# Hybrid decoder block: four rows a visit in the dense stage, a shorter lag, and five edits ahead of it

## The chip, the cores and the metric

The kernel runs on one core of one Trainium2 chip. The metric is device microseconds of one execution, the median of the runs. An execution that the hardware profiler recorded gives the trace; its own time and span stand in the table below. Times in the trace are microseconds from the start of the span.

The engines are called TensorE (PE, and PEld for its weight loads), VectorE (DVE), ScalarE (ACT), GpSimd (POOL) and SyncE (SP); the last three also issue transfers.

## The reference

The layer has 1024 tokens of width 1024, in two sub-layers. Everything is float32.

```python
h = modulate(rms_norm(x, n1_pre), shift1, scale1)
proj = h @ w_in                       # conv gates, q, k, v, o, i, f, g_A, g_B
ya = (b_gate * causal_conv(c_gate * x_in)) @ w_branch_a
ym = (sigmoid(o) * head_norm(mlstm(q, k, v, i, f)) * w) @ w_branch_m
y = (sigmoid(g_A) * ya + sigmoid(g_B) * ym) @ w_out
x = x + gate1 * rms_norm(y, n1_post)

h = modulate(rms_norm(x, n2_pre), shift2, scale2)
q = h @ wq                            # 8 heads, two halves of 128 each
s1, i1 = top_k(q[..., 0] @ subkeys0, 16)      # of 128 keys
s2, i2 = top_k(q[..., 1] @ subkeys1, 16)
sc, e = top_k(all sums s1 + s2, 16)           # 16 of 128 x 128 experts, per head
a = gelu(u[e] . h) * softmax(sc)              # 8 x 16 experts per token
x = x + gate2 * rms_norm(sum_e a_e * v[e], n2_post)
```

u and v are tables of 16384 rows of 1024 values. Each token needs 128 rows of each.

## The kernel before

The tokens stand in two halves of 512. Each goes through the mixer (sub-layer 1) and the scores (query projections and the choice of keys); then the two halves take different roads through the experts. For the first half, rows of u and v are gathered from the tables by indirect transfers. For the second half the experts are computed densely: all 16384 rows of u are projected, the activations are multiplied by a gate matrix G that is zero where a token hasn't chosen an expert, and all rows of v are multiplied with the result.

In time: set-up, the first half's mixer, from 583 us its eight output projections "O", the norm, the first half's scores; from 845 us the second half's mixer with the gathers of the first half underneath; the output projections of the second half end near 1488; a tail with the norm until 1545; the second half's scores until 1752, which also compute 10 of the 40 dense u projections that are done ahead ("az", stored to `A_d`); the selection for the first dense block and the building of the gates (`gates_block`, stored to `G_d`) until 2093; then the dense stage to the end.

**A projection** (`proj_w`, L263) is a group of 24 wide matmuls. A float32 product is split in three passes: high by high, high by low, low by high (L268, L269, L273). `halves` (L246) loads 512 KB of weights into `wr`, ScalarE makes the high part `wh` (L257) and VectorE the low part `wl` (L259). After each matmul `pump` advances the background generator of gathers by `rate[0]` units per projection: RATE1 2.6 at first, RATEM 2 in the middle, RATE1B 4.5 from the M projections of the second half on, RATE2 2.8 and RATE3 3.2 in dense.

**The gathers** (`gather_stream`, L908) alternate u units and v units. A unit issues one indirect transfer of 128 table rows, 512 KB, on POOL's queue (L900 for u, L872 for v) into a buffer that `row_tile` gives: a ring of seven, in the dense stage with three more. `step` keeps the uses in a list and lets the oldest go when what is behind is more than `lag[0]` (LAG 5, in dense LAGD 8). A u use is one VectorE instruction (L905) that multiplies the rows with `h2n` and sums them into a column of `z`. A v use is a visit of TensorE: eight matmul records a row (L891), in four column groups of the array, added into `acc`. v rows are held until `nvs[0]` of them have been issued and then used in one visit: one row per unit would be 1, NVA 2 applies before dense and NV 2 in dense.

```python
            held.append((s, blocks[b].issue_v(s)))
            if len(held) >= nvs[0] or s % 32 == 31:
                step(len(held), lambda z=tuple(held): [blocks[b].use_v(*y) for y in z][-1])
                held.clear()
```

**The order of the work.** Outside dense a list scheduler orders each engine's instructions by their dependences. In dense the order on TensorE, VectorE and ScalarE is written out by hand. There 64 groups of two expert rows each take the rest of the u projections (88), the gelu, the gate from `G_d`, and three passes of v (L1258 to L1260), eight tiles per group; the gather units are pumped in between.

**The mixer's end.** After the last A projection `during(8)` computes the second half's first norm (`norm_mod`: per channel group one scaling, L364, a ScalarE copy, and one subtraction, L368), then VectorE makes `mxh`/`mxl` (L669), the input of the eight O projections. For each O the result is squared (`squares`) and multiplied with the residual input `x2` (`cross`, two projections behind); both are summed by small matmuls into one tile. `turned_sums` (L321) turns the sums, L705 copies them to `m` behind the last issued u use (`last_u`), and the norm goes on.

**The spilled gates.** Eight "gm" projections of the second half are made early, in the first half's tail, where `filler` needs TensorE work, and stored to `spill`. In the second half `gate` loads one into a `t512` buffer (a ring of four of 2 KB) for each of the eight M projections.

**The selection** (`select`, L757) takes for the eight heads the 16 best sums of 50 candidates: adds into `cd`, then per head two rounds of maximum and index (L770 to L776), then turns positions into expert numbers (L803 to L821). `gates_prep` and `gates_block` make one-hots (L1059, L1062), multiply them on TensorE (L1068) and store G. `z_ahead` (L1020) makes the early dense u projections into a buffer "az" that shares tag `W`, of two buffers, with others.

## Time and profile before

| what | value |
|---|---|
| time, median of 3 runs | 3551.16 us (3549.02 to 3554.36) |
| the profiled execution's own time | 3540.15 us |
| its span in the trace | 3538.0 us |
| mean granted clock of TensorE | 0.963 |
| TensorE busy | 3287.7 us, 93% |
| VectorE busy | 2569.6 us, 73% |
| ScalarE busy | 1113.7 us, 31% |
| GpSimd busy | 1182.9 us, 33% |
| moved by transfers | 928.99 MB, mean 263 GB/s |

Busy time is the time in which an engine executes something. Matmuls overlap, so the length printed for one is longer than the distance to the next; the starts are what counts. [...] A page's share is a mean over stages, and what a change is worth is read from the stage in which it is made.

### The profile page before, as it was taken

Reading aid. Unit: us, or ns where it says so; the run is one execution under the profiler, and the core shown is the slowest. Engines: PE = TensorE matmul, PEld = TensorE weight load, DVE = VectorE, ACT = ScalarE, POOL = GpSimd, SP = SyncE. Lnnn points to the kernel's source line nnn. Section 1 sums busy time; section 2 is a strip of 40 time slices with the busy share of each in tenths; the row PEclk is TensorE's granted clock in tenths of the full one; section 3 lists DMA queues with packets and bytes.
Section 4 is the critical chain, followed back from the end, with each engine's and each line's share of the span. In section 5 each row is a group of like instructions: output and inputs, shape, how many; then the busy total and the mean of one; then the engine's idle time right before and its main releaser. Section 6 shows DMA issues by size and latency. Waiting matters only on the chain.

```text
span 3538.0 us, 49527 instructions
## 1 busy us (share of the span) xinstructions
PE 3287.7 (93%) x18208; PEld 2438.1 (69%) x18208; DVE 2569.6 (73%) x6003; ACT 1113.7 (31%) x1831; POOL 1182.9 (33%) x1040
## 2 busy tenths in 40 slices
PE   8999999999988899879968789999999999999997
PEld 5777877686766666446656667777777777776665
DVE  5362444489899886688899848888887888775546
ACT  4442333334332222222256542222222222222221
POOL 0000000001416666546411114544535544444441
PEclk9999999999989899989989899999999999999999
DMA  4226323243739999979957798999989999999994
GB/s 169 84 96 220 121 83 102 83 147 99 276 102 358 333 374 380 355 269 364 345 181 217 217 299 327 352 347 350 344 291 351 349 354 349 352 336 329 320 332 148
DMA packets 326307, 928.99 MB, mean 263 GB/s; under 512 B 35248, under 2 KB 109232, under 8 KB 323888
## 3 DMA queue, kind: packets, MB, share of 16 engines
q0 software_dynamic: 147456, 536.94, 41.5%
q1 hardware_dynamic: 103984, 336.38, 27.1%
q10 hardware_dynamic: 74624, 52.51, 4.8%
q8 instruction: 142, 2.33, 0.3%
q14 instruction: 101, 0.83, 0.1%
HBM read 869.09 MB, written 56.63 MB: 262 GB/s over the span
## 4 chain that ended last, share of the span: by engine, by line
PE 75%; DVE 13%; DMA 5%; issue 3%; ACT 2%; POOL 1%; ACTq 0%; SPq 0%; DVEq 0%; POOLq 0%
PE pj L268 15%; PE pj L269 14%; PE pj L273 14%; PE pa L891 7%; PE pj L1258 5%; PE pj L1259 5%; PE pj L1260 5%; DVE ug L905 2%; PE pm L1258 2%; DMA vg<-in_v_tab_dram,eT 2%; PE pm L1259 2%; PE pm L1260 2%; DVE wl L259 1%; ACT gst L1070 1%; DMA wr<-in_w_in_dram 1%
## 5 line engine op out<-in xcount | busy, mean ns | idle before, releaser
L900 POOL DMA_INDIRECT ug<-in_u_tab_dram,ei x512 | 612.6, 1196 | 1480.6 <-DVE eT L850 869.1
L268 PE MATMUL pj<-hhi,wh 128*128 128x512 f32 x2320 | 950.8, 411 | 39.2 <-ACT wh L257 24.0
L269 PE MATMUL pj<-hlo,wh 128*128 128x512 f32 x2320 | 924.0, 399 | 2.5 <-DVE hlo L368 2.1
L872 POOL DMA_INDIRECT vg<-in_v_tab_dram,eT x512 | 560.8, 1095 | 812.6 <-PE pa L891 513.7
L259 DVE TENSOR_TENSOR wl<-wr,wh 128x512 fp32r<-128x512 f32 x502 | 342.8, 688 | 419.6 <-PE pj L273 352.8
L905 DVE CUSTOM_DVE_ANT_0 ug<-ug,h2n 128x1024 f32<-128x1024 f32 x512 | 615.3, 1222 | 11.5 <-DMA ug<-in_u_tab_dram,ei 9.4
L273 PE MATMUL pj<-hhi,wl 128*128 128x512 f32 x2320 | 600.8, 398 | 6.7 <-DVE wl L259 6.7
L268 PEld LDWEIGHTS pj<-hhi,wh 128*128 128x128 f32 x2320 | 444.6, 192 | 201.7 <-issue 52.8
L257 ACT CAST wh<-wr 128x512 fp32r<-128x512 f32 x502 | 308.7, 621 | 795.5 <-PE pj L269 431.9
L273 PEld LDWEIGHTS pj<-hhi,wl 128*128 128x128 f32 x2320 | 439.6, 191 | 121.2 <-issue 16.4
L269 PEld LDWEIGHTS pj<-hlo,wh 128*128 128x128 f32 x2320 | 445.3, 192 | 101.2 <-DVE hlo L368 8.8
L1242 DVE TENSOR_TENSOR dacc<-dacc,pj 128x512 f32<-128x512 f32 x378 | 256.2, 685 | 297.9 <-PE pj L1260 297.1
L1258 PE MATMUL pj<-Vk,Ak 128*128 128x512 f32 x768 | 308.3, 401 | 11.2 <-ACT Ak L1156 11.1
L891 PE MATMUL pa<-vg,dgm 128*32 128x256 f32 x4096 | 291.5, 390 | 25.7 <-DMA vg<-in_v_tab_dram,eT 23.2
L1260 PE MATMUL pj<-Vk,Ak 128*128 128x512 f32 x768 | 300.1, 391 | 4.1 <-DVE Ak L1159 4.1
L1259 PE MATMUL pj<-Vk,Ak 128*128 128x512 f32 x768 | 301.3, 392 | 0.0
L891 PEld LDWEIGHTS pa<-vg,dgm 128*32 128x32 f32 x4096 | 103.8, 109 | 170.7 <-issue 81.1
L1146 ACT ACTIVATE a<-pj 128x512 f32<-128x512 f32 x88 | 52.6, 598 | 498.1 <-PE pj L273 498.0
L1258 PEld LDWEIGHTS pj<-Vk,Ak 128*128 128x128 f32 x768 | 144.2, 188 | 68.3 <-issue 21.0
L1156 ACT CAST Ak<-a 128x512 fp32r<-128x512 f32 x128 | 79.5, 621 | 353.2 <-DVE a L1154 337.7
L1126 ACT CAST Vk<-vr 128x1024 fp32r<-128x1024 f32 x128 | 134.3, 1049 | 139.6 <-PE pj L1260 128.6
L1260 PEld LDWEIGHTS pj<-Vk,Ak 128*128 128x128 f32 x768 | 144.5, 188 | 37.4 <-DVE Ak L1159 6.1
(324 smaller groups left out, 4145.2 us busy)
## 6 DMA issues: line engine op xcount, KB each, us to landing
wr<-in_w_in_dram SPq DMA_DIRECT2D x128, 512.0 KB, 4.1
wr<-in_uT_dram SPq DMA_DIRECT2D x128, 512.0 KB, 6.2
vr<-in_v_tab_dram SPq DMA_DIRECT2D x128, 512.0 KB, 6.8
gt<-G_d SPq DMA_DIRECT2D x64, 512.0 KB, 8.3
G_d<-gst ACTq DMA_DIRECT2D x15, 2048.0 KB, 11.1
wada<-in_w_ada_dram SPq DMA_DIRECT2D x12, 2048.0 KB, 8.3
wr<-in_wq_dram SPq DMA_DIRECT2D x32, 512.0 KB, 4.1
A_d<-az ACTq DMA_DIRECT2D x40, 256.0 KB, 4.9
```

The costliest lines, as they stand in the source:

```text
L257: S.copy(hi, part)
L259: V.tensor_sub(lo, part, hi.bitcast(F32))
L268: PE.matmul(p, wh, xh[:, dc, :], start=(dc == 0), stop=False)
L269: last_pe[0] = PE.matmul(p, wh, xl[:, dc, :], start=False, stop=False)
L273: last_pe[0] = PE.matmul(p, wl, xh[:, dc, :], start=False, stop=(dc == ND - 1))
L872: G.indirect_dma_start(out=vg, out_offset=None, in_=v_tab, in_offset=bass.IndirectOffsetOnAxis(ap=self.eT[:, t:t + 1], axis=0))
L891: i = PE.matmul(self.acc[32 * q:32 * q + 32, 0:256], self.dgm[t // 8][:, t % 8, :], vg[:, 256 * q:256 * q + 256], start=(tau == 0), stop=( ...
L900: G.indirect_dma_start(out=ug, out_offset=None, in_=u_tab, in_offset=bass.IndirectOffsetOnAxis(ap=self.ei[:, s:s + 1], axis=0))
L905: last_u[0] = order(V.tensor_tensor_reduce(out=ug, in0=ug, in1=self.h2n, scale=1.0, scalar=0.0, op0=OP.mult, op1=OP.add, accum_out=self.z[ ...
L1258: PE.matmul(p, A[:, 0, bs], Vk[:, 0, ds_], start=(i1 == 2 * g), stop=False)
L1259: PE.matmul(p, A[:, 0, bs], Vk[:, 1, ds_], start=False, stop=False)
L1260: PE.matmul(p, A[:, 1, bs], Vk[:, 0, ds_], start=False, stop=(i1 == 2 * g + 1))
```

## The change

Seven edits, of which the first concerns the dense stage and the others the way to it.

1. NV goes from 2 to 4 and LAGD from 8 to 6: in dense four v rows are held and used in one visit, and uses follow six units behind.
2. The two small set-up tiles `diff` and `qd` take buffers of tag `W` in place of `t512`.
3. `norm_mod` gets its loop body as `piece`. The second half's norm no longer stands whole ahead of `mxh`/`mxl`: the O projections 0 to 3 of the first half each take two pieces behind them. In the first half `x2` is loaded after O projection 3 and all eight `cross` come after the last one.
4. The spilled gates are loaded two at a time straight into `u`, ahead of the M projections, in place of one each into `t512`.
5. The rate of the gathers is zero in the last O projection of the second half, and RATE1B again behind it.
6. The selection for the first dense block is made in two halves of four heads (`parts=2`). It is begun in the second half's scores at step 8 and advanced through step 12; the rest follows the scores as before.
7. The "az" buffers are three of their own, in the room of `Cst` (two) and `rstd` (one), in place of two of `W`.

```diff
-NV = 2
+NV = 4
-LAGD = 8
+LAGD = 6
...
+    diff = sp.tile([128, 128], I32, name="diff", tag="W", bufs=2)
-    diff = sp.tile([128, 128], I32, name="diff", tag="t512", bufs=4)
...
-    qd = sp.tile([128, 4, 32], I32, name="qd", tag="t512", bufs=4)
+    qd = sp.tile([128, 4, 32], I32, name="qd", tag="W", bufs=2)
...
-    def norm_mod(x, r, A, sh, keep, in_big=False, first=None):
+    def norm_pieces(x, r, A, sh, keep, in_big=False):
...
-        for dc in range(ND):
-            if first:
-                first(dc)
+
+        def piece(dc):
             s_ = sh[:, dc:dc + 1]
             t = sp.tile([128, TH], F32, name="nm", tag="t512", bufs=4)
             V.scalar_tensor_tensor(t, x[:, dc, :], A[:, dc:dc + 1], r, op0=OP.mult, op1=OP.mult)
...
+        return (hi, lo), hf, piece
...
-        if hf == 1 and (kind, j) in FILL0:
-            nc.sync.dma_start(t, spill[FILL0.index((kind, j))])
-            return t
...
         u = big([128, ND, TH], F32, "u")
+        if hf == 1:
+            for j in range(0, ND, 2):
+                nc.sync.dma_start(u[:, j:j + 2], spill[j:j + 2].rearrange("j p t -> p j t"))
         for j in range(ND):
             wa = ada_load(4 + j) if hf == 0 else None
-            t = gate("gm", j, h, hf)
+            t = gate("gm", j, h, hf) if hf == 0 else u[:, j, :]
...
-        during(8)
         mxh = big([128, ND, TH], F32R, "mxh")
...
-        x2 = big([128, ND, TH], F32, "x2")
-        nc.sync.dma_start(x2, xT[hf])
+        x2s = []
+
+        def x2_load():
+            x2s.append(big([128, ND, TH], F32, "x2"))
+            nc.sync.dma_start(x2s[0], xT[hf])
+
+        if hf == 1:
+            x2_load()
...
         for j in range(ND):
+            if hf == 1 and j == ND - 1:
+                rate[0] = 0.0
             S.copy(y[:, j, :], proj("O", j, (mxh, mxl)))
             squares(j)
-            if j > 1:
+            during(ND + j)
+            if hf == 0 and j == 3:
+                x2_load()
+            if hf == 1 and j > 1:
                 cross(j - 2)
-        cross(ND - 2)
-        cross(ND - 1)
+        if hf == 1:
+            rate[0] = RATE1B
+        for j in range(0 if hf == 0 else ND - 2, ND):
+            cross(j)
...
-    def select(tv, ti, c, res, kind=""):
+    def select(tv, ti, c, res, kind="", parts=1):
...
+        n = H // parts
+        for h0 in range(0, H, n):
+            hs, js = slice(h0, h0 + n), slice(2 * h0, 2 * h0 + 2 * n)
+            V.tensor_copy(i_bf[:, js], ti[:, c, js])
...
+            for hd in range(h0, h0 + n):
+                V.max(sv[:, hd, 0:8], cd[:, hd, :])
+                V.max_index(po[:, hd, 0:8], sv[:, hd, 0:8], cd[:, hd, :])
+                yield 1
...
+            if h0 + n < H:
+                yield 1
...
-            a = sp.tile([128, TD], F32, name="az", tag="W", bufs=2)
+            if not zz:
+                zz.append(sp.tile([128, 2, TD], F32, name="zz", tag="Cst", bufs=1))
+                zz.append(sp.tile([128, 1, TD], F32, name="zy", tag="rstd", bufs=RSB))
+            a = (zz[0][:, 0], zz[0][:, 1], zz[1][:, 0])[n % 3]
...
     def during(j):
...
-        if j == 8:
-            nxt.append(norm_mod(*nxt[0], A1, sh1, False)[0])
+        if j == ND:
+            nxt.extend(norm_pieces(*nxt[0], A1, sh1, False))
+        if ND <= j < ND + 4:
+            nxt[3](2 * (j - ND))
+            nxt[3](2 * (j - ND) + 1)
...
+        if not NX and j == H:
+            chosen.append(select(tv, ti, 0, res0, "d", 2))
+        if not NX and H <= j < H + H // 2 + 1:
+            next(chosen[0])
...
-        for n, _ in enumerate(select(tv, ti, 0, res, "d")):
-            z_ahead(h2, ZT[0] + (ZT[1] - ZT[0]) * (n + 1) / (H + 3))
-        building.append(gates_block(0, *gates_prep(*res)))
+        for n, _ in enumerate(chosen[0]):
+            z_ahead(h2, ZT[0] + (ZT[1] - ZT[0]) * (n + 1) / (H // 2 + 3))
+        building.append(gates_block(0, *gates_prep(*res0)))
```

## Rows read from the trace of the kernel before

**Rows 1.** Busy time on the page: engine, us, share of span, instructions.

```profile
PE 3287.7 (93%) x18208; PEld 2438.1 (69%) x18208; DVE 2569.6 (73%) x6003; ACT 1113.7 (31%) x1831; POOL 1182.9 (33%) x1040
```

**Rows 2.** Windows by stage: busy us of each engine, clock, DMA share, GB/s.

```profile
2150.00:3450.00 1300.00, 1290.58 (x7370) 953.84 (x7369) 982.95 (x1775) 328.69 (x502) 614.20 (x559) 1.00 0.93 340
2660.00:3140.00 480.00, 480.00 (x2676) 359.85 (x2672) 389.43 (x697) 126.61 (x192) 236.10 (x212) 1.00 0.95 350
...
1350.00:1450.00 100.00, 97.41 (x553) 61.68 (x552) 63.78 (x122) 24.95 (x42) 58.66 (x56) 1.00 1.01 388
582.00:600.00 18.00, 10.68 (x35) 7.91 (x34) 14.73 (x24) 8.63 (x15) 0.00 (x0) 0.72 0.39 146
1490.00:1546.00 56.00, 32.65 (x144) 14.34 (x141) 41.22 (x92) 8.57 (x14) 21.88 (x19) 0.70 0.54 183
1545.00:1752.00 207.00, 191.94 (x1179) 136.43 (x1179) 179.63 (x725) 51.01 (x88) 127.32 (x109) 0.99 0.98 366
...
2093.00:2123.00 30.00, 18.91 (x90) 13.04 (x89) 11.42 (x19) 7.93 (x12) 4.95 (x6) 0.77 0.89 334
```

**Rows 3.** Timeline of TensorE around a two-row visit in dense: start, length.

```profile
2281.31 0.39 PE L1259 MATMUL pj<-Vk,Ak 128*128 128x512 f32 x1
...
2282.22 0.39 PE L1260 MATMUL pj<-Vk,Ak 128*128 128x512 f32 x1
2282.54 1.07 PE L891 MATMUL pa<-vg,dgm 128*32 128x256 f32 x16
...
2284.82 0.39 PE L1260 MATMUL pj<-Vk,Ak 128*128 128x512 f32 x1
```

**Rows 4.** Timeline of TensorE around a one-row visit.

```profile
1481.46 0.39 PE L268 MATMUL pj<-mxh,wh 128*128 128x512 f32 x1
1481.78 0.64 PE L891 MATMUL pa<-vg,dgm 128*32 128x256 f32 x8
...
1483.85 0.40 PE L269 MATMUL pj<-mxl,wh 128*128 128x512 f32 x1
```

**Rows 5.** Windows of line L891 alone: the use of v rows in dense.

```profile
2150.00:3450.00 1300.00, 172.38 (x2576) 67.28 (x2576) 1.00 0.93 340
2105.00:3500.00 1395.00, 187.16 (x2784) 72.87 (x2784) 0.99 0.92 333
```

**Rows 6.** DMA issues, 2660 to 3140: count, median us from issue to landing.

```profile
ug<-in_u_tab_dram,ei POOLq DMA_INDIRECT x106, 7.0
vg<-in_v_tab_dram,eT POOLq DMA_INDIRECT x106, 7.3
```

**Rows 7.** Timeline of VectorE at the first half's output projections.

```profile
586.64 2.08 DVE L364 SCALAR_TENSOR_TENSOR nm<-xt,A,rstd 128x512 f32<-128x512 f32 x3
...
590.62 4.91 DVE L669 SCALAR_TENSOR_TENSOR mxl<-u,mxh 128x512 fp32r<-128x512 f32 x8
```

**Rows 8.** Timeline of TensorE there; in brackets idle before, and its releaser.

```profile
587.39 0.80 PE L268 MATMUL pj<-mxh,wh 128*128 128x512 f32 x1 [4.14 <-ACT wh L257]
591.36 0.79 PE L269 MATMUL pj<-mxl,wh 128*128 128x512 f32 x1 [3.17 <-DVE mxl L669]
```

**Rows 9.** Chain of waits through the second mixer's end: start, length, what.

```profile
1490.85 3.12 PE pm L690 x6
...
1494.68 1.05 PE pm L321 x8
```

**Rows 10.** Timeline of VectorE at the same place.

```profile
1506.50 1.23 DVE L905 CUSTOM_DVE_ANT_0 ug<-ug,h2n 128x1024 f32<-128x1024 f32 x1 [3.42 <-DMA ug<-in_u_tab_dram,ei]
...
1507.65 0.17 DVE L705 COPY m<-pm 128x12 f32<-128x12 f32 x1
```

**Rows 11.** Timeline of TensorE at the first dense block's selection.

```profile
1789.24 0.69 PE L1039 MATMUL pm<-ident,e 128*128 128x128 f32 x2 [11.68 <-DVE e L821]
...
1795.50 0.58 PE L1068 MATMUL pj<-oh 128*128 128x128 f16 x4 [4.96 <-DVE oh L1062]
```

**Rows 12.** Waits from 1800 to 2110: total us, times, longest.

```profile
DVE ge L803 <- DMA A_d<-az: 9.7, 3, 5.9
```

More of the change, by code (lines that the diff above doesn't have):

```diff
@@ L355, in norm_mod @@
         else:
[L356 to L357 removed]
+            hi, lo = (hp_.tile([128, ND, TD], F32R, name=n, tag="h") for n in ("hhi", "hlo"))
         hf = big([128, ND, TH], F32, "hf") if keep else None
[L359 to L361 removed]
+        def piece(dc):
             s_ = sh[:, dc:dc + 1]
@@ L368, in norm_mod @@
             V.scalar_tensor_tensor(lo[:, dc, :], t, s_, hi[:, dc, :].bitcast(F32), op0=OP.add, op1=OP.subtract)
-        return (hi, lo) if in_big else whole, hf
+        return (hi, lo), hf, piece
+    def norm_mod(x, r, A, sh, keep, in_big=False, first=None):
+        whole, hf, piece = norm_pieces(x, r, A, sh, keep, in_big)
+        for dc in range(ND):
+            if first:
+                first(dc)
+            piece(dc)
+        return whole, hf
     def x_rms(hf):
@@ L755, in scores @@
                 V.max_index(ti[:, c, j, 8:16], tv[:, c, j, 8:16], r)
-    def select(tv, ti, c, res, kind=""):
+    def select(tv, ti, c, res, kind="", parts=1):
         i_bf = sp.tile([128, 2 * H, TOPK], BF, name="i_bf", tag="i_bf")
-        V.tensor_copy(i_bf, ti[:, c])
-        s1, s2 = tv[:, c, 0::2, :], tv[:, c, 1::2, :]
         cd = sp.tile([128, H, NCAND], F32, name="cd", tag="cd")
-        for a in range(8):
-            V.tensor_add(cd[:, :, OFF[a]:OFF[a + 1]], s2[:, :, 0:CNT[a]],
-                         s1[:, :, a:a + 1].to_broadcast([128, H, CNT[a]]))
-        V.tensor_add(cd[:, :, OFF[8]:NCAND], s1[:, :, 8:16], s2[:, :, 0:1].to_broadcast([128, H, 8]))
@@ L767, in select @@
         sv = sp.tile([128, H, TOPK], F32, name="sv", tag="sv")
         po = sp.tile([128, H, TOPK], U32, name="po", tag="po")
-        for hd in range(H):
-            V.max(sv[:, hd, 0:8], cd[:, hd, :])
-            V.max_index(po[:, hd, 0:8], sv[:, hd, 0:8], cd[:, hd, :])
-            yield 1
-            r = sp.tile([128, NCAND], F32, name="mr2", tag="mr2")
-            V.match_replace(r, sv[:, hd, 0:8], cd[:, hd, :], NEG)
-            V.max(sv[:, hd, 8:16], r)
-            V.max_index(po[:, hd, 8:16], sv[:, hd, 8:16], r)
+        n = H // parts
@@ new lines, in select @@
+        for h0 in range(0, H, n):
+            hs, js = slice(h0, h0 + n), slice(2 * h0, 2 * h0 + 2 * n)
+            V.tensor_copy(i_bf[:, js], ti[:, c, js])
+            s1, s2 = tv[:, c, 2 * h0:2 * h0 + 2 * n:2, :], tv[:, c, 2 * h0 + 1:2 * h0 + 2 * n:2, :]
+            for a in range(8):
+                V.tensor_add(cd[:, hs, OFF[a]:OFF[a + 1]], s2[:, :, 0:CNT[a]],
+                             s1[:, :, a:a + 1].to_broadcast([128, n, CNT[a]]))
+            V.tensor_add(cd[:, hs, OFF[8]:NCAND], s1[:, :, 8:16], s2[:, :, 0:1].to_broadcast([128, n, 8]))
+            for hd in range(h0, h0 + n):
+                V.max(sv[:, hd, 0:8], cd[:, hd, :])
+                V.max_index(po[:, hd, 0:8], sv[:, hd, 0:8], cd[:, hd, :])
+                yield 1
+                r = sp.tile([128, NCAND], F32, name="mr2", tag="mr2")
+                V.match_replace(r, sv[:, hd, 0:8], cd[:, hd, :], NEG)
+                V.max(sv[:, hd, 8:16], r)
+                V.max_index(po[:, hd, 8:16], sv[:, hd, 8:16], r)
+            if h0 + n < H:
+                yield 1
@@ L1009, in block_kernel @@
     A_d = dr.tile([max(ZA, 1), 128, TD], F32, name="A_d")
-    ahead = [0]
+    ahead, zz = [0], []
     NC = -(-TD // TH)
@@ L1324, in filler @@
             gate(*z, h, keep=True)
-    h2, tv, ti = stage1(0, h, lambda h2, j: None, during, filler)
+    h2, tv, ti = stage1(0, h, lambda *z: None, during, filler)
     blocks = []
@@ L1343, in block_kernel, with second @@
     rate[0], mix[0] = RATE1, MIX1
-    building = []
-    def second(h2, j):
+    building, chosen, res0 = [], [], []
+    def second(h2, j, tv, ti):
         z_ahead(h2, ZT[0] * j / 16.0)
+        if not NX and j == H:
+            chosen.append(select(tv, ti, 0, res0, "d", 2))
+        if not NX and H <= j < H + H // 2 + 1:
+            next(chosen[0])
         if NX and j == 4:
```

10 lines of the change are left out of this document (4 added, 6 removed).

## The prediction

> **What bounds the kernel now.** I read the page's busy times first: TensorE is busy in 93% of the span [rows 1]. That is a mean over stages, so the table of windows by stage comes next [rows 2]. In the dense stretch from 2150 to 3450 us TensorE is busy for 1290.58 of 1300 us at a granted clock of 1.00, while the DMA engines stand at a share of 0.93 and 340 GB/s. Between 2660 and 3140 it has no gap at all, and VectorE works 389.43 of 480 us. So in 37% of the span only less TensorE time makes the kernel shorter; nothing that another engine saves there counts. The other windows are the places where TensorE waits and where the clock is granted at half: 582 to 600 (first half's output projections begin), 1490 to 1546 (end of the second mixer) and 2093 to 2123 (dense begins). There it is waits that count, and the timeline around each says which one ends last.
>
> **Four v rows a visit.** In dense every visit to the `acc` accumulation breaks the sequence of wide matmuls. The timeline of a two-row visit shows the price [rows 3]: wide matmuls start every 0.227 us ((2282.22 - 2281.31)/4), and the six steps from 2282.22 to 2284.82 take 2.60 us, where six regular ones take 1.36. The visit costs 1.24 us. A one-row visit [rows 4]: seven steps from 1481.46 to 1483.85 take 2.39 us, regular 1.59, so 0.80. The difference, 0.44, is a row; what is left, 0.36, is paid per visit however many rows it has. Dense has 2784 such matmuls [rows 5], 8 records to a row: 348 rows, 174 visits now, 87 after. 87 x 0.36 = 31.3 us, of which 2576/2784 lie where TensorE is full: 29.0. Reading the row's price as 0.41 or 0.48 moves the fixed part between 0.28 and 0.42, hence 22 to 34 us. I take -29.
>
> [...]
>
> The price of it is in the queue. A visit now waits for the last of four transfers, and the lag falls from eight to six. Tiles in flight are at most ten (six behind plus four held), the ten `row_tile` buffers. Behind a visit of four, u units are used as few as four units after their issue, against eight before. A unit passes every 480/212 = 2.26 us (106 u and 106 v, [rows 6]), so four are 9.1 us. From issue to landing a u row takes 7.0 us and a v row 7.3 (the same rows). The margin is about 2 us, and a late u stalls VectorE, not TensorE. VectorE has 480 - 389.43 = 90.6 us free for 106 u rows, 0.85 us each, before it becomes the bound. I take nothing for it; rival C has the other end.
>
> **First half's output projections.** Now `during(8)` puts sixteen norm instructions of VectorE (three take 2.08 us, [rows 7]) ahead of `mxh`/`mxl`. TensorE stands 4.14 and then 3.17 us, the second wait ending with `mxl` [rows 8]. In the window of 18 us 35 matmuls start, at a mean clock of 0.72 [rows 2]; at 0.227 us apart they need 7.9, so 10 us are lost. With the norm in pieces behind the O steps, 2 x 2 x 0.69 = 2.8 us of VectorE a step hide under a projection of 24 x 0.227 = 5.4 us. `mxl` stays ahead of the second matmul (8 x 0.61 us, [rows 7]), so some 3 us remain lost: -7. If the scheduler orders the wait elsewhere, 0.
>
> The other end of that stage gets longer. `x2` is loaded at j == 3, so all eight `cross` come after the last projection: a pass cost 3.12/6 = 0.52 us at half clock [rows 9], two of the eight stood there already, and six less 1 us that leaves the loop is +2. Net -5, from -9 to 0.
>
> **Spilled gates in place.** Eight loads of 256 KB become four of 512 KB into `u`, issued before the M projections. The u buffer is free only when what had its slot is read; the loads replace a `t512` buffer for each projection. M in the second half is paced by VectorE's u rows (1.23 us each, [rows 10]), so 0, from -3 to +3.
>
> **Rate 0 in the last O projection of the second half.** `m` (L705) is ordered behind the last u row. That u row ran at 1506.50, and `m` at 1507.65, though the sums had left TensorE by 1494.68 + 1.05 = 1495.73 [rows 9, 10]: 11.9 us in which TensorE mostly stands (32.65 busy of 56, [rows 2]). Without 4.5 units in that projection the last u is some two rows earlier, near 1499, and the chain starts there: -8. Should the list scheduler place other u rows there, -2; all of it is -12. The four and a half units go to dense, two v rows of 0.44 us, and two one-row visits of 0.80 leave the O projection; that is even.
>
> **First dense block chosen in halves.** Today TensorE waits 11.68 us for `e` and 4.96 for the one-hots [rows 11]. Half of the heads' work moves into the scores. The gain is bounded below by nothing and above by both waits, 16.6 us; the steps from L803 to L821 and the one-hots stay where they are, behind the second four heads, so I take a good half less than the first wait, -5, and -10 as the good end. In the scores window VectorE has 27 us free of 207 and TensorE 15 [rows 2], and 5 us more work is partly on the path: +1, from 0 to +4.
>
> **Own buffers for `az`; `diff` and `qd` in `W`.** `ge` (L803) waits 9.7 us in three waits for `az` transfers that hold `W` [rows 12]; with three buffers of their own those vanish. They overlap partly with the wait above: -3, from -8 to 0. Moving `diff` and `qd` costs no instruction. It moves the pool's layout, and the first dense buffers meet other tenants; the window in which dense starts already stands 11 us idle [rows 2] waiting for a transfer, so I take 0, from -6 to +3.
>
> **Sum.** -29 - 5 - 8 - 5 + 1 - 3 = -49 us. The profiled execution took 3540.15 us, 11.0 less than the median of the runs, 3551.16. 3540.15 - 49 = 3491, 1.4% less; of the median, 3502.
>
> **Rivals.** (A) *The transfers set dense.* If rows come no faster than now, a shorter TensorE sequence only waits for them, and dense gives nothing: -20, 3531. Against it: the same queues moved 388 GB/s between 1350 and 1450 us, at a share of 1.01, with dense at 350 [rows 2]. [...] 7%.
>
> (B) *Dense gains, the front doesn't.* Outside dense a list scheduler orders the instructions, and each of the five front edits removes a wait that could be taken by the next: the weights' transfer, `wh`, or the scores' VectorE. Then -29, 3522. The waits removed are of VectorE behind something that isn't needed, which speaks against. 20%.
>
> (C) *u rows come late* (slower). Place: VectorE in dense, at the u row issued four units before its use. Stretching 2150 to 3140 holds 106/480 x 990 = 219 u rows. If each waits w us, what is over 0.85 lengthens dense: the 49 us are gone at w = 0.85 + 49/219 = 1.07; w = 1.3 gives 3502 + 99 = 3601. Landing would have to go from 7.0 to over 10 us on average. It speaks for it that the DMA engines are at 0.95 there; against it that issue runs ahead whenever a buffer is free. 7%.
>
> (D) *The visits' price is per row.* Were the 0.36 us a wait for the rows that a longer visit pays as well, dense saves nothing, and the rest stands: 3531, as in A. Both shown visits came with no idle time, so 4%.
>
> **How the numbers follow.** My forecast, both gains, 62%; B 20%; A 7%; D 4%; C 7%. The predicted time is 3502. Its own range is 3475 (34 in dense, the front's good ends) to 3520; to leave out no more than 2 in 10, the range reaches up over B to 3532, near A and D, and down to 3475. About 0.2%, 7 us, is what a measurement of this kernel can tell from no change. A, B and D are faster by 19 to 29 us; with their spread, one in twelve of them and of the forecast ends within 7 us. Faster 0.86, within 0.07, slower 0.07.
>
> **What would show it.** Right: in dense half as many visits, each with x32 matmuls and some 2.0 us from the last wide start to the next; the stretch of full TensorE shorter by about 29 us; the idle 3.17 us before `mxl` gone or smaller; `m` within 3 us of the end of L321; the wait before `e` under 8 us; `ge` no more behind `az`. Wrong: VectorE idle before L905 behind its transfer in dense, TensorE idle before L891 behind four transfers, a wait of `cross` for `x2`, or a first dense load that is later than before.

## The result and the profile after

The changed kernel took 3507.54 us, median of 4 runs (3501.86 to 3516.24); the kernel before, in the same comparison, 3550.09 (3548.51 to 3554.36). The ratio is 0.9881, with an interval from 0.986 to 0.9901: 42.6 us less, where 49 were forecast, and 5.5 us from the predicted time. The profiled execution of the changed kernel took 3504.27 us, its span is 3502.4.

Line numbers after differ: the use of v rows is L916 (L891 before), of u rows L930 (L905), the three passes of v L1286 to L1288 (L1258 to L1260), the low part of Ak L1187 (L1159), the copy `m` L725 (L705), the cross products L702 (L690). First the busy times on the page, which answer to [rows 1]: TensorE works 19 us less, and the shares stay within a point.

```profile
PE 3268.7 (93%) x18208; PEld 2459.3 (70%) x18208; DVE 2569.4 (73%) x6013; ACT 1114.5 (32%) x1831; POOL 1177.2 (34%) x1040
```

The windows by stage, as in [rows 2]: the stretch from 2150 to 3450 for comparison, then the first half's output projections, the end of the second mixer, and the second half's scores.

```profile
2150.00:3450.00 1300.00, 1281.21 (x7553) 981.37 (x7552) 987.60 (x1799) 330.86 (x506) 614.61 (x562) 0.99 0.94 342
582.00:600.00 18.00, 16.68 (x62) 11.30 (x63) 13.33 (x22) 9.55 (x17) 0.00 (x0) 0.91 0.28 80
1474.00:1530.00 56.00, 39.27 (x189) 18.85 (x185) 43.00 (x94) 11.56 (x18) 19.91 (x19) 0.76 0.61 214
1530.00:1755.00 225.00, 201.51 (x1174) 143.27 (x1175) 182.84 (x772) 51.26 (x88) 125.08 (x109) 0.95 0.93 338
```

The beginning of the output projections is nearly full now (16.68 of 18 us busy, before 10.68). The tail has 17 us idle in 56, before 23. The scores are worse: 225 us with the clock at 0.95, where before 207 sufficed. And dense, where TensorE had next to no gap, has 19 us of idle time in 1300, before 9.

The timeline of TensorE at four places: first O projection, the cross products, the first selection, a four-row visit.

```profile
582.90 0.50 PE L269 MATMUL pj<-mxl,wh 128*128 128x512 f32 x1 [1.15 <-DVE mxl L675]
...
645.04 0.40 PE L268 MATMUL pj<-hhi,wh 128*128 128x512 f32 x1
645.36 1.04 PE L702 MATMUL pm<-xy,gw 128*32 128x512 f32 x2
646.34 0.50 PE L269 MATMUL pj<-hlo,wh 128*128 128x512 f32 x1
646.68 0.40 PE L268 MATMUL pj<-hhi,wh 128*128 128x512 f32 x1
...
1785.71 0.69 PE L1067 MATMUL pm<-ident,e 128*128 128x128 f32 x2 [8.65 <-DVE e L846]
...
1791.12 0.59 PE L1096 MATMUL pj<-oh 128*128 128x128 f16 x4 [4.11 <-DVE oh L1090]
...
2710.87 1.07 PE L273 MATMUL pj<-hhi,wl 128*128 128x512 f32 x4
2711.87 1.93 PE L916 MATMUL pa<-vg,dgm 128*32 128x256 f32 x32
2713.73 1.20 PE L273 MATMUL pj<-hhi,wl 128*128 128x512 f32 x4
2714.76 0.39 PE L1286 MATMUL pj<-Vk,Ak 128*128 128x512 f32 x1
```

The wait for `mxl` is 1.15 us, before 3.17 [rows 8]. The waits for `e` and for the one-hots are 8.65 and 4.11, before 11.68 and 4.96 [rows 11]. The visit: from 2710.87 to 2714.76 eight wide matmuls start, which need 1.82 us of the 3.89, so it costs 2.07; 4 x 0.44 + 0.36 was forecast, 2.12.

What the time went into is read best from the trace by stretches, from one marked instruction to the next. "O to m" runs from the last copy of an O projection of the second half to the copy `m`, "scores" from there to the last first-round maximum of the scores (L750, after L770), "choice" to the first copy of expert numbers (`eT`), "gates" to the first copy of a v tile (`Vk`), "u part" from the 9th to the 97th of these 128 copies, "v part" on to the last. One execution each, in us; "after" is the changed kernel, and e1 to e12 are the runs of the next section.

| kernel | O to m | scores | choice | gates | u part | v part | median of runs |
|---|---|---|---|---|---|---|---|
| before | 19.8 | 241.7 | 40.4 | 313.7 | 936.8 | 383.1 | 3550.1 |
| after | 10.0 | 259.4 | 34.4 | 302.8 | 935.0 | 367.7 | 3507.5 |
| e1, four rows alone | 18.6 | 246.3 | 38.8 | 312.1 | 954.7 | 364.9 | 3545.9 |
| e2, after, even uses | 10.1 | 256.6 | 36.9 | 304.1 | 925.8 | 367.8 | 3503.0 |
| e3, after, rate kept | 17.7 | 250.7 | 36.6 | 300.7 | 953.2 | 364.7 | 3532.7 |
| e4, after, cross in loop | 10.0 | 258.4 | 33.1 | 308.4 | 948.3 | 368.7 | 3521.1 |
| e5, after, two rows | 10.0 | 256.5 | 34.0 | 301.6 | 938.5 | 387.0 | 3533.6 |
| e6, four rows alone, even | 19.0 | 247.0 | 37.1 | 321.3 | 931.1 | 367.0 | 3518.4 |
| e7, four rows alone, shifted | 19.1 | 247.4 | 38.1 | 313.9 | 943.5 | 368.8 | 3537.1 |
| e8, before, shifted | 18.7 | 245.6 | 39.1 | 314.5 | 939.1 | 387.0 | 3547.7 |
| e9, after, low part early | 10.0 | 257.1 | 35.5 | 306.2 | 931.0 | 367.4 | 3509.2 |
| e10, e2 and e9 together | 10.0 | 258.2 | 36.8 | 310.1 | 919.6 | 367.4 | 3504.0 |
| e11, after, az in W | 10.0 | 256.8 | 34.5 | 309.3 | 938.2 | 367.7 | 3521.7 |
| e12, after, choice whole | 10.0 | 254.8 | 37.8 | 307.2 | 938.0 | 367.6 | 3513.6 |

These are single executions, and they scatter. The kernel before, e1, e6, e7 and e8 have the same code up to dense, and their "gates" take 312.1 to 321.3 us; the changed kernel, e2, e5, e9 and e10 have the same code up to there, and theirs take 301.6 to 310.1.

Two readings. The v part, where u rows run only in the first 50 us (the last u use is at 3165.83 before, 3145.78 after), is 15.4 us shorter with four rows: 1184 matmul records of L891 there, 74 visits against 37, 0.42 us each (against e5 19.3 us, 0.52 each). The u part holds more visits (1488 records, 93 visits) and should have gained 46 x 0.42 = 19 us; it gained 2. That is the first question. The second: the tail won 9.8 us, and the scores behind it lost 17.7.

For the first question the u part can be taken apart. The table has its length, the time in which TensorE is idle, and the time in which the granted clock, a share of TensorE's full speed, stood at the lower of two levels: the traces of the kernel before and of the changed one record it at 1.00 or at 0.50 and at nothing else. The last column takes from the length the idle time and half of the time at 0.50, where wide matmuls start 0.43 us apart in place of 0.23 (the timeline of e1 below); it is an estimate of what the work takes at a clock of 1.00.

| kernel | u part | TensorE idle | at the lower clock | rest |
|---|---|---|---|---|
| before, two rows | 936.8 | 9.2 | 3.4 | 925.9 |
| e5, two rows | 938.5 | 7.0 | 10.2 | 926.4 |
| e1 | 954.7 | 29.0 | 27.3 | 912.0 |
| e7 | 943.5 | 24.2 | 20.5 | 909.1 |
| after | 935.0 | 18.7 | 13.7 | 909.5 |
| e6 | 931.1 | 14.0 | 20.5 | 906.9 |
| e2 | 925.8 | 12.1 | 10.2 | 908.5 |
| e10 | 919.6 | 7.1 | 10.2 | 907.4 |

So against the kernel before the visits of four save 14 to 19 us of work in each of the six kernels of the table that have them, in e1 too. What differs between the kernels is how much of it idle time and the clock take back.

### The profile page after: what moved, and what is told of

It reads as the page before. It is cut to its first block, busy times and chain, and to the rows that moved or that the text cites. A ratio compares the mean times of both kernels' runs of the same rounds, so it can differ in the third digit from the quotient of the medians.

```text
span 3502.4 us, 49498 instructions
## 1 busy us (share of the span) xinstructions
PE 3268.7 (93%) x18208; PEld 2459.3 (70%) x18208; DVE 2569.4 (73%) x6013; ACT 1114.5 (32%) x1831; POOL 1177.2 (34%) x1040
## 3 DMA queue, kind: packets, MB, share of 16 engines
q0 software_dynamic: 147456, 536.94, 41.9%
q1 hardware_dynamic: 103920, 336.38, 27.3%
## 4 chain that ended last, share of the span: by engine, by line
PE 69%; DVE 15%; DMA 7%; issue 5%; ACT 2%; POOL 1%; ACTq 1%; SPq 0%; POOLq 0%; DVEq 0%
PE pj L268 14%; PE pj L269 13%; PE pj L273 13%; PE pa L916 6%; PE pj L1286 4%; PE pj L1288 4%; PE pj L1287 4%; DVE ug L930 3%; DMA vg<-in_v_tab_dram,eT 2%; PE pm L1286 1%; PE pm L1287 1%; PE pm L1288 1%; DVE wl L259 1%; DMA wr<-in_uT_dram 1%; ACT gst L1098 1%
## 5 line engine op out<-in xcount | busy, mean ns | idle before, releaser
L897 POOL DMA_INDIRECT vg<-in_v_tab_dram,eT x512 | 553.0, 1080 | 799.0 <-PE pa L916 531.2
L930 DVE CUSTOM_DVE_ANT_0 ug<-ug,h2n 128x1024 f32<-128x1024 f32 x512 | 612.0, 1217 | 12.1 <-DMA ug<-in_u_tab_dram,ei 10.2
L1286 PE MATMUL pj<-Vk,Ak 128*128 128x512 f32 x768 | 305.8, 398 | 14.9 <-ACT Ak L1184 11.6
L1288 PE MATMUL pj<-Vk,Ak 128*128 128x512 f32 x768 | 301.5, 393 | 14.7 <-DVE Ak L1187 14.7
L916 PE MATMUL pa<-vg,dgm 128*32 128x256 f32 x4096 | 273.2, 387 | 20.2 <-DMA vg<-in_v_tab_dram,eT 19.9
L916 PEld LDWEIGHTS pa<-vg,dgm 128*32 128x32 f32 x4096 | 112.8, 110 | 148.7 <-issue 63.5
L1286 PEld LDWEIGHTS pj<-Vk,Ak 128*128 128x128 f32 x768 | 144.7, 188 | 63.5 <-issue 15.4
L1288 PEld LDWEIGHTS pj<-Vk,Ak 128*128 128x128 f32 x768 | 144.8, 189 | 49.6 <-DVE Ak L1187 19.5
L1287 PEld LDWEIGHTS pj<-Vk,Ak 128*128 128x128 f32 x768 | 144.9, 189 | 29.8 <-DVE Vk L1157 1.4
```

The costliest lines, as they stand in the source:

```text
L897: G.indirect_dma_start(out=vg, out_offset=None, in_=v_tab, in_offset=bass.IndirectOffsetOnAxis(ap=self.eT[:, t:t + 1], axis=0))
L916: i = PE.matmul(self.acc[32 * q:32 * q + 32, 0:256], self.dgm[t // 8][:, t % 8, :], vg[:, 256 * q:256 * q + 256], start=(tau == 0), stop=( ...
L930: last_u[0] = order(V.tensor_tensor_reduce(out=ug, in0=ug, in1=self.h2n, scale=1.0, scalar=0.0, op0=OP.mult, op1=OP.add, accum_out=self.z[ ...
L1286: PE.matmul(p, A[:, 0, bs], Vk[:, 0, ds_], start=(i1 == 2 * g), stop=False)
L1287: PE.matmul(p, A[:, 0, bs], Vk[:, 1, ds_], start=False, stop=False)
L1288: PE.matmul(p, A[:, 1, bs], Vk[:, 0, ds_], start=False, stop=(i1 == 2 * g + 1))
```

## The experiments

Each kernel was compared with the kernel before in five rounds; the ratios are to its runs on the same chip (medians 3549.4, 3545.7 and 3548.8 us in the three comparisons, e1 to e4, e5 to e8, e9 to e12).

**Four rows alone (e1).** The kernel before with the first edit only.

```diff
-NV = 2
+NV = 4
-LAGD = 8
+LAGD = 6
```

> The kernel before with NV 4 and LAGD 6 and none of the other edits. Theory of the prediction (0.36 us saved at each of 87 visits): 29 us less than before, about 3521 us. Rival, read from the trace of the changed kernel, in which dense takes 22 us less than before (1407 to 1385): part of the gain is lost to the low parts Ak that VectorE makes late, because the pops behind a visit of four come in bursts of u rows; then 20 us less, about 3530 us, with TensorE idle before the third pass of v (line L1260 of the kernel before) some ten times for 1 to 2 us, and nearly all of the gain after the last u row. A rival that says the visits matter only in the last part, where no u rows are left: 15 us less, 3535.

Measured: 3545.89 us, ratio 0.9993 (0.9982 to 1.0005). By itself the edit that carried 29 of the 49 us forecast gains nothing that can be told. All three expectations had a larger gain. The v part won 18 us (1.8 of them because four v rows fewer fall into it), the u part lost 18. The table of waits from 2170 to 3130 us, TensorE only (total, times, longest), of the kernel before, of this kernel and of the changed one:

```profile
PE pj L1260 <- DVE Ak L1159: 4.1, 3, 2.5
```

```profile
PE pj L1260 <- DVE Ak L1159: 20.8, 13, 3.0
```

```profile
PE pj L1288 <- DVE Ak L1187: 14.0, 10, 1.9
```

One such wait, on VectorE's timeline of the run:

```profile
2825.76 0.76 DVE L1154 TENSOR_TENSOR a<-a,gt 128x256 f32<-128x256 f32 x2
2826.43 1.22 DVE L1129 TENSOR_TENSOR Vk<-vr,Vk 128x1024 fp32r<-128x1024 f32 x1
2827.57 1.22 DVE L905 CUSTOM_DVE_ANT_0 ug<-ug,h2n 128x1024 f32<-128x1024 f32 x1
...
2828.71 1.22 DVE L905 CUSTOM_DVE_ANT_0 ug<-ug,h2n 128x1024 f32<-128x1024 f32 x1
...
2829.86 0.68 DVE L1242 TENSOR_TENSOR dacc<-dacc,pj 128x512 f32<-128x512 f32 x1
2830.45 0.69 DVE L1159 TENSOR_TENSOR Ak<-a,Ak 128x512 fp32r<-128x512 f32 x1
```

and on TensorE's:

```profile
2827.70 0.49 PE L1259 MATMUL pj<-Vk,Ak 128*128 128x512 f32 x1
2831.20 0.80 PE L1260 MATMUL pj<-Vk,Ak 128*128 128x512 f32 x1 [3.00 <-DVE Ak L1159]
2831.79 0.63 PE L268 MATMUL pj<-hhi,wh 128*128 128x512 f32 x1
...
2836.48 0.55 PE L269 MATMUL pj<-hlo,wh 128*128 128x512 f32 x1
2836.87 0.40 PE L268 MATMUL pj<-hhi,wh 128*128 128x512 f32 x1
```

VectorE gates an expert row (L1154), makes the low part of Vk (L1129), then two u uses, a sum, and only then Ak's low part, for which TensorE waits 3.00 us. What follows costs nearly as much again: the next twelve wide matmuls, from 2831.79 on, start 0.43 us apart and not 0.23, until 2836.87. The two u uses stand together because a visit of four counts four units: appending it pushes the sum over the lag, and `step` lets several u uses go at once.

No row was late at this place. In the whole window VectorE waited 4.9 us for u rows in e1, and more, 6.9 us, in e6, which has the gain (e1 first):

```profile
DVE ug L905 <- DMA ug<-in_u_tab_dram,ei: 4.9, 3, 2.9
```

```profile
DVE ug L905 <- DMA ug<-in_u_tab_dram,ei: 6.9, 5, 3.3
```

So late rows are not what e1 loses by. NV and LAGD were not changed one without the other.

**Even uses (e2).** The changed kernel, in dense each use popped six units behind its issue, not when the sum passes the lag.

```diff
-            pend.append((n, use))
-            while sum(z[0] for z in pend) > lag[0]:
-                pop()
+            pend.append((n, use, unit[0] + LAGD))
...
+        def due():
+            while nvs[0] == NV and pend and pend[0][2] <= unit[0]:
+                pop()
```

> The changed kernel with each use in dense placed a fixed six units behind the last issue of its rows, so that u uses come one by one and no two of them stand behind one another at a visit. Visits of four stay. Theory (bursts of u rows make Ak late): TensorE's waits before L1288 in the u part of dense, 14 us in ten waits, go to under 4, the stretch from the first group without stall to the last u row takes 15 to 20 us less, total 15 to 20 us below the changed kernel. Rival (VectorE simply has too little time left, however its work is placed): within 5 us of the changed kernel. Rival (rows come too late at a distance of six units): waits of VectorE or TensorE behind the row transfers, and longer than the changed kernel.

Measured: 3502.95 us, ratio 0.9876 (0.9857 to 0.9894), by the intervals the same as the changed kernel. In the trace the u part is 9 us shorter (925.8 against 935.0) and the waits for Ak are 8.0 us in nine:

```profile
PE pj L1301 <- DVE Ak L1200: 8.0, 9, 1.8
```

So the direction is as the theory says, the size is half of what was expected, and the total doesn't show it: it is as the first rival had it, within 5 us.

**Rate kept (e3).** The changed kernel without edit 5.

```diff
-            if hf == 1 and j == ND - 1:
-                rate[0] = 0.0
...
-        if hf == 1:
-            rate[0] = RATE1B
```

> The changed kernel without the rate of zero in the last O projection of the second half. Theory of the prediction (the copy of the sums stands behind a u row that this projection issued): the copy comes 8 to 10 us later against the end of that projection, and the total is 8 us above the changed kernel. Rival, read from the trace of the changed kernel: the tail's 10 us are given back in the scores behind it, since the gather units that were put off run there and take transfers and VectorE time; then the total is within 3 us of the changed kernel and the scores take 8 to 10 us less.

Measured: 3532.71 us, ratio 0.9951 (0.9935 to 0.9967): 25 us more, three times what the prediction said, and far from the rival's 3. The tail lost 7.7 and the scores gave 8.7 back, as the rival said. But the u part took 953.2 us, as in e1. The instructions of VectorE stand in dense in exactly the order of e1, and not in that of the changed kernel: 4.5 gather units more before dense, and each burst of u uses meets another place of the groups.

**Cross products in the loop (e4).**

```diff
+            for k in {5: (0, 1), 6: (2, 3, 4), 7: (5, 6)}.get(j, ()) if hf == 0 else ():
+                cross(k)
...
-        for j in range(0 if hf == 0 else ND - 2, ND):
+        for j in range(ND - 1 if hf == 0 else ND - 2, ND):
```

> The changed kernel with seven of the eight cross products of the first half moved back into the O loop, behind the squares of O 5 (two), O 6 (three) and O 7 (two); x2 is still loaded after O 3 and the norm still goes by pieces. Theory (a pass in 128x32 tiles costs TensorE about 1.2 us where it breaks a run of wide matmuls alone, as six times after the loop, and nearly nothing beside the squares, which use other column groups): the copy of the sums comes 6 to 7 us after the last O is copied in place of 15, total 6 to 8 us below the changed kernel. Rival (the wait for x2, 2 MB loaded from O 3 on, takes the place): O 5 or O 6 lengthens by what is saved, total within 2 us of the changed kernel.

Measured: 3521.12 us, ratio 0.9925 (0.9906 to 0.9944): the stage did as expected and the kernel got slower. The copy of the sums comes 7.1 us after the last O copy in place of 15.3, the O loop is 2.6 longer, and the first half's second norm begins 4.9 us earlier than in the changed kernel. None of that is left at the beginning of dense, which is 5 us later. And dense itself takes longer though the instructions of all five engines stand there in the order of the changed kernel. What differs is which matmul VectorE's sums wait for (waits from 2170 to 3130 us, first the changed kernel, then this one):

```profile
DVE dacc L1270 <- PE pm L1288: 4.3, 3, 2.1
DVE ug L930 <- DMA ug<-in_u_tab_dram,ei: 1.2, 4, 0.4
```

```profile
DVE dacc L1272 <- PE pm L1290: 23.3, 9, 4.7
```

In the one group compared, a sum that waits for the following tile as well comes 1.8 us later, the low part of Ak behind it too. Why these waits differ between two programs with one order stays open. So with one order the u part has taken 935.0 us (changed kernel) and 948.3 (e4), and the order alone doesn't settle what dense takes.

**Two rows in the changed kernel (e5).** `NV = 2` and `LAGD = 8` in the changed kernel.

> The changed kernel with NV back at 2 and LAGD back at 8: the six edits ahead of dense alone. In the profile of the changed kernel dense begins 14 us earlier than before, and dense itself takes 21 us less. Theory (the two parts add up, 14 from the front and the rest from the visits): 3535 to 3537 us, 28 us above the changed kernel, although four rows alone in the kernel before gained nothing. Rival (the visits give nothing in the changed kernel either, and the front's edits have all the gain): within 6 us of the changed kernel.

Measured: 3533.63 us, ratio 0.9954 (0.9937 to 0.997), as the first theory said. The six other edits are worth 16 us, four rows on top of them 26. Yet four rows in the kernel before were worth 2.5. TensorE's waits for Ak are as few here as in the kernel before (4.1 us in three waits there):

```profile
PE pj L1288 <- DVE Ak L1187: 4.3, 5, 1.6
```

**Even uses in the kernel before (e6).** e1 with the edit of e2.

> The kernel before with four rows a visit and each use six units behind its issue, none of the other edits. Four rows alone stood TensorE 20.8 us in thirteen waits for the low parts Ak, and lost 18 us from the first groups to the last u row where two rows a visit lose nothing. Theory (u rows that come two and three at a time right ahead of the low parts eat what the visits save): the waits for Ak fall below 9 us, the loss below 5, total 20 to 30 us under the kernel before, 3520 to 3530. Rival (four rows a visit and a lag of six lose it by something else, such as rows that come late): as four rows alone, 3546, within 6 us.

Measured: 3518.44 us, ratio 0.9916 (0.9899 to 0.9934). This goes far to answer the first question: the same visits of four, the same lag of six, the same front, and 27 us less than e1, with the u uses spread. The u part falls from 954.7 to 931.1, of which 15 us are idle time of TensorE. In VectorE's order in the u part there are 87 low parts of Ak; three or more u uses stand between the gating of a row and its low part at three of them in the kernel before, at eleven in e1, and at one here. The edit moves the visits too, so that the place of the uses in a group, which the next run is about, changes along with the bursts; how much of the 27 us is due to it is not shown. The waits are halved:

```profile
PE pj L1273 <- DVE Ak L1172: 10.6, 9, 4.1
```

**The place in the group (e7, e8).** 4.5 units taken from the credit at the beginning of dense, with four rows (e7) and with two (e8).

```diff
             nvs[0] = NV
+            bg[1] -= 4.5
```

> The kernel before with NV 4 and LAGD 6, and 4.5 gather units taken from the credit at the beginning of dense, about what the rate of zero in the last O projection puts off. Nothing else is changed, so that the uses meet other places of the groups. Theory (the loss hangs on where the bursts of u uses fall in a group of two expert rows): in dense as in the changed kernel, 14 to 22 us under four rows alone, 3524 to 3532. Rival (the place does not matter): as four rows alone, 3546, within 5 us. Rival (fewer units at the start help by themselves): then two rows a visit with the same 4.5 units gain as well.

> The kernel before with the 4.5 units taken from the credit at the beginning of dense and nothing else; two rows a visit. Control for the run before. Theory (pops of two rows come evenly at any place of the group): within 5 us of the kernel before. Rival (the units put off help by themselves, at the crowded beginning of dense): 8 us or more under the kernel before.

Measured: e7 3537.14 us, ratio 0.997 (0.9959 to 0.9982); e8 3547.68, ratio 1.0003 (0.9989 to 1.0016). With two rows the shift is worth nothing; with four it is worth 8 us, of the 14 to 22 expected. The intervals of e7 and e1 just touch, so the 8 us that e7 has over e1 are barely clear of the noise. If they are real, the place of the bursts matters, and is a part of what the changed kernel has over e1. It isn't by fewer bursts: e7 and the changed kernel both have three or more u uses ahead of a low part twelve times, e1 eleven times. And the waits for Ak in e7 are nearly those of e1:

```profile
PE pj L1260 <- DVE Ak L1159: 19.6, 12, 3.0
```

Its order of VectorE's instructions in dense is near that of the changed kernel, not the same.

**Low part early (e9), and with even uses (e10).**

```diff
-                    [do(a_gate, d1), do(v_lo, d1)],
-                    [do(a_lo, d1)],
+                    [do(a_gate, d1), do(v_lo, d1), do(a_lo, d1)],
+                    [],
```

> The changed kernel with the low part Ak of the second expert row of a group made one step earlier, right behind the low part of Vk, so that no u use is pumped between the gating of this row and its low part. Theory (u uses that stand ahead of Ak's low part make TensorE wait, and the wait is followed by a stretch at half clock): TensorE's waits for Ak in the u part of dense fall from 14 us to under 4, total 8 to 15 us below the changed kernel, 3493 to 3500. Rival (VectorE is late as a whole there, and what it does first only moves the wait to another input): the waits for Ak go, waits for VectorE's sums or Vk come in their place, total within 5 us of the changed kernel.

> The changed kernel with both: each use six units behind its issue, and Ak's low part of the second row one step earlier. Theory: the waits for Ak nearly vanish, dense takes what two rows a visit take less 87 visits of 0.44 us, 38 us; against the changed kernel with two rows a visit (3534) that is 3496, and 3490 to 3497 with the scatter of the part ahead. Rival (even uses have taken all there is): as even uses alone, 3503, within 4 us.

Measured: e9 3509.22 us, ratio 0.9893 (0.9875 to 0.991); e10 3504.01, ratio 0.9866 (0.9849 to 0.9883). In e9 the waits for Ak are gone, and others come, as its rival said; in e10 both are small (the same table of waits, e9 first):

```profile
PE pj L268 <- DVE dacc L1270: 9.3, 7, 1.6
PE pj L1286 <- DVE dacc L1270: 4.4, 2, 3.5
```

```profile
PE pj L1299 <- DVE dacc L1283: 4.1, 2, 3.2
PE pj L268 <- DVE dacc L1283: 2.2, 3, 1.1
```

In e10 the u part takes 919.6 us, 17.2 less than before, near the 19 that 46 visits fewer are worth. But the "gates" stretch of that execution was 7 us longer, and the total is that of e2, as the rival said. e10 has the lowest ratio of all, with an interval that overlaps the changed kernel's; a version that is shown to beat it wasn't found.

**az back in W (e11)** undoes edit 7.

```diff
-            a = (zz[0][:, 0], zz[0][:, 1], zz[1][:, 0])[n % 3]
+            a = sp.tile([128, TD], F32, name="az", tag="W", bufs=2)
```

> The changed kernel with the az tiles back in the two buffers of tag W. From the selection's end to the beginning of dense the kernel before took 314 us in the traces and the changed kernel 303. Theory (the three own buffers make this difference: VectorE's steps of the selections no longer wait for az transfers): 314 us again in this stretch, total 8 to 14 us above the changed kernel. Rival, the prediction's own price: 3 us above. Rival (the difference comes from another edit): within 2 us in this stretch.

Measured: 3521.66 us, ratio 0.9926 (0.9911 to 0.994), 14 us above the changed kernel, and the intervals are apart. The prediction gave this edit 3 us. Where the time is lost is not shown. The "gates" stretch is 309.3 us, 6.5 longer than in the changed kernel, but within the 301.6 to 310.1 that the same code with buffers of its own takes; and no `ge` waits for `az` in it, though the theory rests on that wait. Another 5.7 us stand between the first `Vk` copy and the ninth (79.4 against 73.7; in e2 76.8), 3.2 in the u part.

**The choice whole again (e12)** undoes edit 6.

```diff
-        if not NX and j == H:
-            chosen.append(select(tv, ti, 0, res0, "d", 2))
-        if not NX and H <= j < H + H // 2 + 1:
-            next(chosen[0])
```

> The changed kernel with the first dense block's selection whole and behind the scores again, as before. The scores of the second half, from the copy of the sums to the last one, took 242 to 247 us in the kernel before and its dense variants, 251 in the changed kernel without the rate of zero, 256 to 259 with it. Theory (half of the selection in the scores costs them some 5 us of VectorE, and saves 4 between the scores and the first expert numbers): the scores take 250 to 254, the stretch behind them 38 to 40, total within 3 us of the changed kernel. Rival (the halves save what the prediction says, 5 us, and cost 1): 4 us above the changed kernel. Rival (the scores' loss is all of this edit): the scores take 242 to 247 and the total is 8 us below.

Measured: 3513.64 us, ratio 0.9897 (0.988 to 0.9913): 6 us above the changed kernel, the intervals overlap. The choice takes 37.8 us in place of 34.4, the scores 254.8 in place of 259.4, so that the two stretches together are no longer than in the changed kernel.

## Why the prediction was right

**The price of a visit** held. 0.36 us per visit was read from two visits; the v part gives 0.42 to 0.52, the work of the u part 0.30 to 0.41 (the last column of the table above, 14 to 19 us for 46 visits), a visit of four costs 2.07 where 2.12 was computed, and e6 against the kernel before gives 30 us for 29.

**"I take nothing for it"** is the step that failed, although the total came out. The prediction weighed late rows (rival C) and found a margin of 2 us. Late rows weren't the loss: in the changed kernel VectorE waited for u rows 1.2 us from 2170 to 3130, and e6 waits longer for them than e1. What was missed is the order on VectorE. The mean of 0.85 us that VectorE has free for each u row is no margin for two or three u uses in a row ahead of an input that TensorE is about to need. e1 shows the step's full price, the whole gain: 14 us of work saved in the u part, 20 us of idle time and some 12 of clock lost. e6 shows that it is the way the uses are spread; e3 and e7 suggest that it depends on where in a group the bursts fall, though e4 loses 13 us in the u part with the changed kernel's own order. In the changed kernel edit 5 seems to move them to a better place, and 22 us are left in the profiled execution (from the first pass of v to the last 1407 us, after 1385). That e1 and e5 add up to 19 us and the changed kernel has 43 is explained by e7 only in part (8 us); the rest stays open.

**The output projections.** The first part was right: from the last matmul of the A projections to the end of the last O copy it is 57.7 us for 64.7, 7 less as forecast. The other end was mis-sized. The prediction gave the cross products behind the loop 0.52 us a pass, +2 in sum; from the last O copy to `m` it took 8.2 us more. The timeline above shows a pass by itself: two records between wide matmuls at 645.04 and 646.34, and an extra 0.11 behind, 1.18 us for one product; six of them are 7.1 us. Beside the squares the same product had cost 0.1 us. This is a visit of squares and product before, and one of squares alone after:

```profile
627.09 0.40 PE L269 MATMUL pj<-mxl,wh 128*128 128x512 f32 x1
...
627.54 0.62 PE L690 MATMUL pm<-xy,gw 128*32 128x512 f32 x1
...
628.51 0.50 PE L268 MATMUL pj<-mxh,wh 128*128 128x512 f32 x1
```

```profile
612.08 0.40 PE L269 MATMUL pj<-mxl,wh 128*128 128x512 f32 x1
...
613.40 0.50 PE L268 MATMUL pj<-mxh,wh 128*128 128x512 f32 x1
```

From wide start to wide start it is 1.42 us with the product and 1.32 without. Reckoned like the 1.18, the squares alone cost 1.20: a visit of one product costs TensorE as much as one of two squares in two column groups. So the term of the sum that was mis-sized is the six products, 8 us and not 2. Net the stage gained nothing where -5 was forecast, and e4 confirms it for the stage.

**The rate of zero.** The tail won 9.8 us, 8 forecast: the copy runs right behind the last u use, 3.4 us after the sums have left TensorE (the chain of waits first, then VectorE).

```profile
1487.96 1.05 PE pm L321 x8
```

```profile
1491.27 1.22 DVE L930 CUSTOM_DVE_ANT_0 ug<-ug,h2n 128x1024 f32<-128x1024 f32 x1
...
1492.41 0.17 DVE L725 COPY m<-pm 128x12 f32<-128x12 f32 x1
```

Here too the end that was left out of the sum is larger. The scores took 9 to 18 us more (241.7 to 247.4 in the five executions with the front of the kernel before, 256.5 to 259.4 in the five with that of the changed kernel), +1 forecast. e3 puts 6 to 9 of it on the rate, e12 2 to 5 on the choice; the rest is open. It isn't the units put off: the scores of the changed kernel hold 57 u uses and 58 v rows, those of e3 56 and 58, and dense gets 243 and 352 for 241 and 348, as the prediction said. Four of the 6 to 9 us stand between the copy `m` and the first maximum (46.1 us, in e3 41.9); why is not shown. One place where the scores lose time: SyncE's queue, ScalarE and TensorE at 1635 to 1648 us.

```profile
1635.27 2.31 SPq L1025 DMA_DIRECT2D out_dram<-oq  x4
1637.62 1.01 SPq L1010 DMA_DIRECT2D x2q<-x2n_d  x2
1638.73 0.40 SPq L251 DMA_DIRECT2D wr<-in_uT_dram  x1
```

```profile
1646.70 0.62 ACT L257 CAST wh<-wr 128x512 fp32r<-128x512 f32 x1 [7.59 <-DMA wr<-in_uT_dram]
```

```profile
1647.86 2.07 PE L768 MATMUL pm<-sk,qv 128*128 128x128 f32 x8 [3.60 <-ACT qv L763]
```

Four stores of `oq` stand in SyncE's queue until VectorE has made them, a wait of 4.3 us, and the load of the next weights (L251) behind them goes out at 1638.73. ScalarE waits 7.59 us for it, TensorE 3.60 for ScalarE. The prediction named no queue there. But this place is an example, not the cause: the kernel before has the same four stores at 1640.23, and ScalarE waits 4.89 us for weights behind them; over the whole scores ScalarE waits less for weights in the changed kernel than in e3 (33.6 us and 42.6).

**The choice** gained 3 us in its own stretch where 5 were forecast, and cost 2 to 5 in the scores where 1 was; the 6 us of e12's total are within the noise. **Own buffers for az** were worth more, 14 us in e11 for 3, and no wait shows where. **The spilled gates** were put at nothing, and nothing can be told: executions of one and the same program ahead of dense differ by 10 us in the second half's mixer (after and e5, from 849.9 to 1482.4 and from 850.8 to 1493.3).

So the six edits of the front gave 16 us for the 20 forecast, with three of the terms (output projections, scores, az) wrong by 5 to 17 us and of both signs, and four rows gave 26 for 29 only in the changed kernel, for reasons that the prediction hadn't looked at and that are known in part. Taken back one by one with four rows in dense, edits 5, 7 and 6 cost 25, 14 and 6 us, more than the 16 of all six with two rows: some of what they do is done in dense. Edits 2 and 4 were not tested alone. Of the prediction's own signs, two fell just short: `m` came 3.4 us behind the end of L321 (3), and the wait before `e` is 8.65 (8). The range held by luck as much as by reason: terms that were wrong offset each other.

## What to carry to other kernels

Where one engine takes its work in bursts, a mean of free time per item can hide the loss (here 0.85 us free for each u row, and 20.8 us of waits for Ak in e1): look for which input of the bound engine stands behind the longest burst, and move the input, or spread the burst, before crediting the gain. Price small matmuls by the visit in which they stand: here a cross product that cost 0.1 us beside the squares cost 1.18 us when the same change gave it a visit of its own between wide matmuls. An edit that shifts the place of a background stream can change what follows it (4.5 units later: 8 us in e7 with four rows, barely clear of the noise, and nothing in e8 with two); test it with the stream shifted and nothing else changed. And compare single executions of one program before reading a few us of a stretch as an effect.

## What was unexpected in the hardware

The wait of 3.00 us in e1 was not paid once. After it the matmuls start 0.43 us apart for 5 us, at the lower level of the clock (granted 0.50 from 2829.98 to 2836.81), which loses 2.4 us more (12 x 0.20, an estimate from the starts); after a wait of 1.56 us in the changed kernel they go on at a clock of 1.00 (starts 0.23 us apart):

```profile
2635.97 0.50 PE L1288 MATMUL pj<-Vk,Ak 128*128 128x512 f32 x1 [1.56 <-DVE Ak L1187]
2636.31 0.39 PE L268 MATMUL pj<-hhi,wh 128*128 128x512 f32 x1
2636.54 0.40 PE L269 MATMUL pj<-hlo,wh 128*128 128x512 f32 x1
```

Length alone doesn't decide it here. In the changed kernel TensorE waited 1.84 us twice: up to 2292.78, and the matmuls went on 0.23 us apart, and up to 2761.52, and from 2762.70 to 2765.69 wide ones stood 0.43 us apart (granted 0.50 from 2762.36 to 2765.77). In the u part of e1 the clock is at its lower level for 27.3 us in all, in e6 for 20.5. So of the 23.6 us by which e6's u part is shorter, 15 are idle time and about 3 are the clock; the rest, 5, holds four v rows fewer and is otherwise not explained.
